# First stage of a hybrid attention layer: wider modulation steps, unmodulated staging of x, and normalization one block ahead

## The chip, the cores and the metric

The kernel runs on one core of a Trainium2 chip. The metric is the device time of one launch in microseconds; smaller is better. The kernel before was timed in three runs: median 3094.35 us, from 3090.94 to 3095.23 us. One further execution was profiled. Engines are named as the profile names them: PE multiplies matrices (PEld loads its stationary operand), DVE, ACT and POOL work element by element, SP issues nearly all transfers (its queue is SPq; ACT has a queue of its own, ACTq).

## The reference

One decoder layer over 2048 tokens of width 1024, in float32:

```
mod = silu(c) @ w_ada + b_ada                    # 6 x 1024 columns: shift_a, scale_a, gate_a, ...
h   = rms_norm(x, g_attn) * (1 + scale_a) + shift_a
proj = h @ w_in                                  # q|k|v of 8 FoX heads, q|k|v of 8 stick-breaking heads, 8 forget logits
...                                              # both attentions, head norms
x = x + gate_a * (mix @ w_out)
...                                              # gated MLP with a width-3 causal convolution
out = rms_norm(x, g_final)
```

The change touches the first three lines alone. For them, `mod` needs only the first 2048 columns of `w_ada` (shift and scale, 8 MB), `h` needs all 1024 features of a token for its norm, and every projection needs `h` of all features.

## The kernel before, in words

Tokens go in four blocks of 512 (`TB`), features in eight tiles of 128 (`KT`; kt counts them). Products are made with operands split in a rounded high part and the remainder (`split`, L43: ACT writes the high part on L44, POOL or DVE the low part on L45), so that one product is three matmuls.

The attention runs over 32 units (kind, pair of heads, token block), `units` on L648: stick-breaking ("sb") pairs first, then FoX. While a unit attends (`attend`), the projection of later units is worked off as a filler, so PE has both kinds of work; `pace` and `follow` set how fast. The four units of ("sb", 0) are special: their projection also makes `h`. `norm_proj` (L417) loads a block of x, normalizes it, transposes it, applies the modulation, splits the result into `hp` tiles, multiplies, and stores `hp` to memory (`hs`) for the other pairs. Block 0 of ("sb", 0) is drained before any attention starts (L770): that is the first stage. The tool that builds the program orders the instructions of each engine itself; each engine then runs its own in that order, and an instruction that waits holds all behind it on its engine. The transfers of SP and ACT together take turns with eight completion semaphores, so each transfer waits for the one that used its semaphore eight transfers earlier.

In the first stage, for each kt in turn:

- `mod_cols(kt)` (L206) loads both 128-column stripes of `w_ada` (L209, two transfers of 512 KB in runs of 512 bytes), scales five of the eight row groups by silu(c) and adds them up on DVE (L212, L214), scales three on ACT (L216) and adds them on POOL (L218); PE sums over the partitions with eight LDWEIGHTS and one-column matmuls (L223), and DVE writes one column each of shift and scale (L224, L225) into `mod_a`.
- `w[1](kt)` loads one 128 x 256 piece of the raw q|k weights through a ring of three buffers (L258, L259) and splits it, the low part on DVE.
- `modulate` (L100) transposes four tiles of x on PE (L114), and ACT reads them from PSUM with the scale and shift of this kt (L119), so these transposes' banks are held until the modulation is known. The split puts `hp`'s low part on DVE in block 0 and on POOL in the later blocks.
- `done` stores `hp` (L430) and adds three matmuls for q and three for k (L284).

After kt 7 come the v weights (L259, L44, L45) and the v product (L355, 96 matmuls in four groups of 24), q and k are copied out of PSUM (L314, L315, L330) and sent to their attention layout by eight transfers (L319, L334). `steps_of_values` (L391) writes v to memory, reads it back shifted by one token (L399), and subtracts.

For blocks 1 to 3, the x loads stand ahead of `modulate` (L658), and the first step of the generator squares (ACT, L95), takes the root (L96), the reciprocal (DVE, L97) and scales (L106) all four tiles, just before that block's transposes.

## Time and profile before

| what | us |
|---|---|
| median of three runs | 3094.35 |
| profiled execution, as timed | 3089.98 |
| its span, first to last instruction | 3088.3 |
| PE busy | 2951.0 |
| DVE busy | 2075.5 |
| ACT busy | 1682.6 |
| POOL busy | 992.2 |

In the profile, "busy" counts an engine's instructions without the waits between them. A row of the timeline gives start, duration, engine, line, operation and, in brackets, how long the engine had been idle and what it waited for. A row of a windows view gives the busy time and the instruction count of PE, PEld, DVE, ACT and POOL in a stretch of time, then the clock that PE was granted (1.00 is full), the busy share of the transfer engines and GB/s. The first query and key matmuls of the attention start at 72.19 us, the transposes of block 1 at 79.19 us, those of block 2 near 121 us and those of block 3 at 185.45 us.

### The profile page before, as it was taken

What the parts mean: (1) busy time and instruction counts of PE and PEld (TensorE: products, weight loads), DVE (VectorE), ACT (ScalarE), POOL (GpSimd) and SP (SyncE); (2) the same over time, 40 slices, a digit from 0 to 9 for tenths busy, and PEclk for the clock granted to TensorE, in tenths of its full rate; (3) what the DMA queues carried; (4) which work ended last, traced back from release to release, by engine and by line L of the source; (5) the groups of instructions that cost most, each with busy time, mean ns of one, the idle gap of its engine ahead of it and who ended that gap; (6) DMA issues with size and microseconds to landing.
All of it is one profiled execution on the core that took longest, in us unless ns stands there. A gap on an engine that the chain in (4) does not pass through costs nothing.

```text
span 3088.3 us, 45418 instructions
## 1 busy us (share of the span) xinstructions
PE 2951.0 (96%) x15934; PEld 2510.9 (81%) x15934; DVE 2075.5 (67%) x3206; ACT 1682.6 (54%) x3129; POOL 992.2 (32%) x1011
## 2 busy tenths in 40 slices
PE   6889999999999999999998999999899998999998
PEld 5788888888888897888876788888688887888887
DVE  6768878887876667578634687778877776254243
ACT  5657767776776656568534444444444444333332
POOL 1531322143122422321123344444444442332331
PEclk8999999999999999999999999999999999999999
DMA  9648756776579855956167522222322224555562
GB/s 272 229 134 293 239 191 202 289 230 202 183 235 341 269 191 184 303 188 224 59 214 226 187 85 82 82 82 76 92 76 82 82 82 155 183 199 167 183 204 86
DMA packets 310614, 546.80 MB, mean 177 GB/s; under 512 B 30737, under 2 KB 187153, under 8 KB 309361
## 3 DMA queue, kind: packets, MB, share of 16 engines
q1 hardware_dynamic: 298752, 531.27, 53.0%
q10 hardware_dynamic: 11632, 12.63, 1.2%
q8 instruction: 126, 2.06, 0.3%
q14 instruction: 104, 0.84, 0.1%
HBM read 407.14 MB, written 130.36 MB: 174 GB/s over the span
## 4 chain that ended last, share of the span: by engine, by line
PE 57%; DMA 12%; DVE 12%; POOL 7%; issue 7%; ACT 4%; SPq 1%; POOLq 0%; ACTq 0%; DVEq 0%
PE ps_pj L284 8%; PE ps_o L1084 8%; PE ps_pv L461 7%; PE ps_pt L452 6%; PE ps_pj L355 5%; PE ps_t L1084 4%; PE ps_bc L1084 4%; PE ps_qk L442 3%; PE ps_o L746 3%; PE ps_o L934 3%; PE ps_qk L443 3%; DMA wuraw<-in_w_up_dram 3%; DVE wu L45 3%; DVE u L1003 2%; POOL wuraw L921 2%
## 5 line engine op out<-in xcount | busy, mean ns | idle before, releaser
L934 PE MATMUL ps_o<-oa,wu 128*128 128x512 f32 x2088 | 504.1, 392 | 11.9 <-DVE oa L45 6.0
L934 PEld LDWEIGHTS ps_o<-oa,wu 128*128 128x128 f32 x2088 | 390.8, 188 | 102.5 <-DVE oa L45 9.8
L457 DVE TENSOR_TENSOR at<-ps_pt,at 128x512 fp32r<-128x512 f32 (+1 forms) x576 | 365.6, 651 | 101.8 <-ACT at L456 98.5
L284 PE MATMUL ps_pj<-hp,w_qk 128*128 128x512 f32 x1512 | 421.1, 406 | 13.3 <-DMA hp<-hs 7.6
L480 DVE TENSOR_TENSOR_SCAN a<-r,a 128x512 f32<-128x512 f32 (+2 forms) x320 | 374.0, 1186 | 86.3 <-POOL a L477 45.1
L461 PE MATMUL ps_pv<-at,V 128*128 128x256 f32 x2304 | 406.3, 293 | 17.4 <-DVE at L457 6.3
L456 ACT ACTIVATE at<-ps_pt 128x512 fp32r<-128x512 f32 (+1 forms) x576 | 318.9, 576 | 157.2 <-PE ps_pt L452 123.6
L461 PEld LDWEIGHTS ps_pv<-at,V 128*128 128x128 f32 x2304 | 335.8, 191 | 54.1 <-DVE at L457 19.7
L284 PEld LDWEIGHTS ps_pj<-hp,w_qk 128*128 128x128 f32 x1512 | 274.5, 191 | 65.4 <-DMA hp<-hs 8.7
L45 DVE TENSOR_TENSOR wd<-wdraw,wd 128x1024 fp32r<-128x1024 f32 x88 | 114.1, 1297 | 261.6 <-ACT wd L44 261.5
L442 PE MATMUL ps_qk<-K,Q 128*128 128x512 f32 (+2 forms) x640 | 264.7, 414 | 11.4 <-ACT a L475 6.0
L1084 PE MATMUL ps_o<-wd,g 128*128 128x512 f32 x1040 | 250.7, 391 | 8.7 <-ACT g L44 8.7
L45 POOL TENSOR_TENSOR g<-graw,g 128x512 fp32r<-128x512 f32 x84 | 144.6, 1722 | 323.4 <-ACT g L44 309.3
L934 PE MATMUL ps_t<-ob,wu 128*128 128x512 f32 x984 | 241.6, 390 | 0.0
L355 PE MATMUL ps_pj<-w_v,hp 128*128 128x256 f32 (+1 forms) x1536 | 237.1, 290 | 2.6 <-DVE w_v L45 1.3
L44 ACT ACTIVATE wu<-wuraw 128x512 fp32r<-128x512 f32 x214 | 133.2, 626 | 190.7 <-PE ps_o L934 120.5
L1084 PEld LDWEIGHTS ps_o<-wd,g 128*128 128x128 f32 x1040 | 196.1, 189 | 49.9 <-ACT g L44 9.1
L443 PE MATMUL ps_qk<-K,Q 128*128 128x512 f32 (+2 forms) x640 | 236.1, 370 | 0.0
L355 PEld LDWEIGHTS ps_pj<-w_v,hp 128*128 128x128 f32 x1536 | 211.8, 192 | 12.4 <-DVE q L315 2.1
L934 PEld LDWEIGHTS ps_t<-ob,wu 128*128 128x128 f32 x984 | 185.4, 188 | 38.7
L44 ACT ACTIVATE wd<-wdraw 128x1024 fp32r<-128x1024 f32 x88 | 93.1, 1058 | 206.2 <-PE ps_bc L1084 190.9
L474 ACT ACTIVATE r<-ps_qk 128x512 f32<-128x512 f32 (+2 forms) x320 | 172.5, 540 | 60.4 <-PE ps_qk L443 58.4
(222 smaller groups left out, 5504.3 us busy)
## 6 DMA issues: line engine op xcount, KB each, us to landing
hp<-hs SPq DMA_DIRECT2D x224, 512.0 KB
wuraw<-in_w_up_dram SPq DMA_DIRECT2D x84, 512.0 KB
wdraw<-in_w_down_dram SPq DMA_DIRECT2D x84, 512.0 KB
g<-u SPq DMA_DIRECT2D x42, 512.0 KB
graw<-g SPq DMA_DIRECT2D x84, 256.0 KB
hs<-hp SPq DMA_DIRECT2D x32, 512.0 KB
hp<-in_w_ada_dram SPq DMA_DIRECT2D x32, 512.0 KB
qk_fox<-q SPq DMA_DIRECT2D x32, 512.0 KB
```

The costliest lines, as they stand in the source:

```text
L44: nc.scalar.activation(hi, src, AF.Copy)
L45: (lo_engine or nc.gpsimd).tensor_sub(lo, src, f(hi))
L284: nc.tensor.matmul(acc, w[kt][:, a, n], h[:, bb], start=kt == 0 and i == 0, stop=kt == KT - 1 and i == 2)
L355: nc.tensor.matmul(av[:, t * width:(t + 1) * width], hts[kt][:, a, tok], w[1][kt][:, bb, 0:width], start=kt == 0 and m == 0, stop=kt == KT ...
L442: nc.tensor.matmul(b[:, :cw], Q[:, hl, 0, qcols], K[:, hl, :cw], start=True, stop=False)
L443: marks.append(nc.tensor.matmul(b[:, :cw], Q[:, hl, 1, qcols], K[:, hl, :cw], start=False, stop=True).ins)
L456: nc.scalar.activation(at[:, 0, lo:], b[:, lo:], AF.Copy)
L457: nc.vector.tensor_sub(at[:, 1, lo:], b[:, lo:], f(at[:, 0, lo:]))
L461: nc.tensor.matmul(o[:, 0:2 * P], V[kt // 4][:, kt % 4, hl, :], rhs, start=first and kk == 0 and w == 0, stop=last and kk == 1 and w == 1)
L480: nc.vector.tensor_tensor_scan(rev, r[:, 0:need][:, ::-1], rev, 0.0 if right[qi] is None else right[qi][:, 0:1], ALU.mult, ALU.add)
L934: nc.tensor.matmul(b, w[:, p, j], o[:, q], start=first and i == 0, stop=last and i == 2, skip_group_check=True)
L1084: nc.tensor.matmul(banks[t][n], g[:, a, t * P:(t + 1) * P], w[:, b, n * TB:(n + 1) * TB], start=k == 0 and i == 0, stop=k == NKD - 1 and i ...
```

## The change

Block 0 gets a function of its own, `first_block`, and the normalization of block n+1 is started inside block n.

- **Modulation in four steps.** `load_ada(g)` loads 256 columns each of shift and scale in eight transfers of 256 KB with runs of 1024 bytes; the first two of four groups have eight own buffers, the third sits in the two Q buffers, the fourth in two `at` and two `q2` buffers. `mod_cols(g)` scales three row groups on ACT (L256), adds them on POOL (L258), and DVE adds the other five onto that sum (L261). There are four one-column matmuls per step, and shift and scale of two kt at once.
- **All loads up front.** The loads of x, all of `w_ada`, the raw q|k weights, the raw v weights (both in V buffers) and x of block 1 are written in a row, none waiting for a buffer of the first stage. The small loads of `wfr` and `b_fgate` move from SP's queue to ACT's.
- **x staged unmodulated.** All 32 transposes of block 0 are copied to SBUF (K buffers) as they are, on ACT and DVE in turn (L468, L466); ACT applies the modulation from there (L476).
- **Low parts.** The low parts of the first pair's weights move from DVE to POOL; in blocks 1 to 3, every second `hp` low part moves from POOL to DVE.
- **Late stores.** The `hp` tiles of block 0 are stored after the stage: three behind the k transfers, five behind the read-back of v.
- **Normalization ahead.** `begin_block(tb + 1)` loads and normalizes the next block; for block 1 behind the v weights, for blocks 2 and 3 behind the last step of `modulate` of the block before.

The core of the diff:

```diff
+    def begin_block(tb, step=TB // P):
+        xts = load_x(tb)
+        junk = f(sb.tile([P, 2, 2 * 2 * P], F32R, name="at", tag="at", bufs=3)).rearrange("p a n -> p (a n)")
+        normalize(px, xts, "a", junk, step)
+        blocks.append(xts)
...
+            for k in range(2):
+                r = (2 * m + k) * P
+                nc.sync.dma_start(w[:, k], w_ada[r:r + P, 0:2 * D].rearrange("p (i n) -> p i n", i=2)[
+                    :, :, g * 2 * P:(g + 1) * 2 * P])
...
+    nc.scalar.dma_start(wfr, w_in[:, 6 * 512:6 * 512 + NH].rearrange("(k p) n -> p k n", p=P))
+    for t in range(4):
+        nc.scalar.dma_start(bf_c[t * NH:(t + 1) * NH], b_fgate.rearrange("o n -> n o"))
+    begin_block(0, 1)
+    load_ada(0)
+    raw_qk = load_raw(3 * 512, 4)
+    raws = {"qk": next(raw_qk)}
+    load_ada(1)
+    next(raw_qk)
+    load_ada(2)
+    load_ada(3)
+    raw_v = load_raw(3 * 512 + 1024, 1)
...
-    def mod_cols(kt):
-        w = sm.tile([P, KT, 2, P], F32, name="ada", bufs=3)
-        for i in range(2):
-            nc.sync.dma_start(w[:, :, i], w_ada[:, i * D + kt * P:i * D + (kt + 1) * P].rearrange(
-                "(k p) n -> p k n", p=P))
...
+    def mod_cols(g):
+        w = [adas[4 * g + k // 2][:, k % 2] for k in range(KT)]
+        for k in range(3):
+            nc.scalar.activation(w[k], w[k], AF.Copy, scale=cs[:, k:k + 1])
+            if k:
+                nc.gpsimd.tensor_add(w[0], w[0], w[k])
+        t = sm.tile([P, 2, 2 * P], F32, name="adas", bufs=1)
+        for k in range(3, KT):
+            nc.vector.scalar_tensor_tensor(t, w[k], cs[:, k:k + 1], w[0] if k == 3 else t, ALU.mult, ALU.add)
...
+    def first_block(w):
+        xts = blocks[0]
+        stage = [sb.tile([P, 2, TB], F32, name="xT", tag="K", bufs=5) for _ in range(KT // 2)]
+        for kt in range(KT):
+            b = pt()
+            for i, xt in enumerate(xts):
+                nc.tensor.transpose(b[:, i * P:(i + 1) * P], xt[:, kt * P:(kt + 1) * P], ident)
+            if kt % 2:
+                nc.vector.tensor_copy(stage[kt // 2][:, kt % 2], b)
+            else:
+                nc.scalar.activation(stage[kt // 2][:, kt % 2], b, AF.Copy)
+        aq, ak = pj(), qk()
+        hts = []
+        for kt in range(KT):
+            w[1](kt)
+            if kt % 2 == 0:
+                mod_cols(kt // 2)
+            hf = px.tile([P, TB], F32, name="hf_a", bufs=2)
+            nc.scalar.activation(hf, stage[kt // 2][:, kt % 2], AF.Identity, scale=mod_a[:, 0, kt:kt + 1],
+                                 bias=mod_a[:, 1, kt:kt + 1])
+            h = h_tile()
+            split(h[:, 0], h[:, 1], hf, nc.vector)
+            hts.append(h)
+            accumulate(aq, 0, w[0], h, kt)
+            accumulate(ak, 1, w[0], h, kt)
+        w[1:] = [w[2]()]
+        begin_block(1)
+        g = finish_proj("sb", 0, 0, aq, w, hts, ak)
+        next(g)
+        with tc.issue_after(copied[-1]):
+            for kt in range(3):
+                nc.sync.dma_start(hs[0][kt], f(hts[kt]))
+        drain(g)
+        with tc.issue_after(fetched[-1]):
+            for kt in range(3, KT):
+                nc.sync.dma_start(hs[0][kt], f(hts[kt]))
...
+        yield
+        yield from modulate(px, pt, blocks[tb], mod_a, lambda kt: h_tile(), done, "a", True)
+        if tb + 1 < NTB:
+            begin_block(tb + 1)
+        yield from finish_proj("sb", 0, tb, aq, w, hts)
```

Three places of the order that the change makes, each before and then now.

**ACT's first instructions** (`rows`: gains and biases; `wfr`, `bf_c`: the small loads; `at<-xt` on L95: the square of a tile of x; names in brackets: what is waited for, DMAHW being the eight completion semaphores). Before:

```order
L196 DMA rows_306<-in_g_out_fox_dram 4x128
L196 DMA rows_306<-in_g_out_sb_dram 4x128
L196 DMA rows_306<-in_b_ada_dram 48x128 [waits DMAHW1_49]
L95 ACTIVATE at_333,ss_a_334<-xt_315 128x1024 [waits DMAHW2_49]
L96 ACT_TABLE_LOAD [waits DVE_49]
L96 ACTIVATE ss_a_334<-ss_a_334,epsc_275 128x1 [waits Activation_49]
L95 ACTIVATE at_333,ss_a_339<-xt_316 128x1024 [waits DMAHW4_49]
```

Now:

```order
L229 DMA rows_306<-in_g_out_sb_dram 4x128
L229 DMA rows_306<-in_b_ada_dram 48x128 [waits DMAHW1_49]
L231 DMA wfr_312<-in_w_in_dram 128x8x8 [waits DMAHW3_49]
L233 DMA bf_c_282<-in_b_fgate_dram 8x1 [waits DMAHW5_49]
L233 DMA bf_c_282<-in_b_fgate_dram 8x1 [waits DMAHW7_49]
L233 DMA bf_c_282<-in_b_fgate_dram 8x1 [waits DMAHW1_49]
L233 DMA bf_c_282<-in_b_fgate_dram 8x1 [waits DMAHW3_49]
L95 ACTIVATE at_326,ss_a_327<-xt_318 128x1024 [waits DMAHW2_49]
L256 ACTIVATE ada_347<-ada_347,cs_279 128x512 [waits DMAHW2_49,Activation_49]
```

Five transfers, each with a wait for an earlier transfer, now stand ahead of ACT's first square; they left SP's queue, where they stood ahead of the first `w_ada` load.

**ACT around the last `hp` tiles of block 0** (`hf_a`: modulated x; `hp`: its high part; `w_v`: the split of the v weights; `at<-xt`: squares of block 1). Before:

```order
L119 ACTIVATE hf_a<-ps_pt,mod_a 128x512
L44 ACTIVATE hp<-hf_a 128x512
L216 ACTIVATE ada<-ada,cs 128x256 x3
L95 ACTIVATE at,ss_a<-xt 128x1024
L455 ACTIVATE at<-edge 128x2x128 x2
L95 ACTIVATE at,ss_a<-xt 128x1024
L119 ACTIVATE hf_a<-ps_pt,mod_a 128x512
L95 ACTIVATE at,ss_a<-xt 128x1024
L44 ACTIVATE hp<-hf_a 128x512
L95 ACTIVATE at,ss_a<-xt 128x1024
```

Now:

```order
L476 ACTIVATE hf_a<-xT,mod_a 128x512 x2
L44 ACTIVATE w_v<-raws 128x256
L44 ACTIVATE w_v<-wfr 128x8
L44 ACTIVATE w_v<-raws 128x256
L44 ACTIVATE hp<-hf_a 128x512
L95 ACTIVATE at,ss_a<-xt 128x1024
L44 ACTIVATE hp<-hf_a 128x512
L525 ACTIVATE at<-edge 128x2x128 x2
L95 ACTIVATE at,ss_a<-xt 128x1024
L476 ACTIVATE hf_a<-xT,mod_a 128x512 x2
L95 ACTIVATE at,ss_a<-xt 128x1024
L44 ACTIVATE hp<-hf_a 128x512 x2
```

The v weights, of which six stand ahead of the first row shown, and three squares of block 1 now come ahead of kt 6 and 7.

**PE at the end of the first stage** (`ps_pj<-w_v,hp`: the v product; `ps_qk<-K,Q`: the first attention matmuls). Before:

```order
L355 MATMUL ps_pj<-w_v,hp 128x264 x39
L442 MATMUL ps_qk<-K,Q 128x256
L443 MATMUL ps_qk<-K,Q 128x256
L442 MATMUL ps_qk<-K,Q 128x256
L443 MATMUL ps_qk<-K,Q 128x256
L355 MATMUL ps_pj<-w_v,hp 128x264 x48
```

Now:

```order
L325 MATMUL ps_pj<-hp,w_qk 128x512 x2
L325 MATMUL ps_qk<-hp,w_qk 128x512 x2
L396 MATMUL ps_pj<-w_v,hp 128x264 x73
L512 MATMUL ps_qk<-K,Q 128x256
L513 MATMUL ps_qk<-K,Q 128x256
```

The first attention matmuls stood between two halves of the v product; they now follow all of it.

More of the change, by code (lines that the diff above doesn't have):

```diff
@@ new lines @@
+    wfr = sm.tile([P, KT, NH], F32, name="wfr")
+    nc.scalar.dma_start(wfr, w_in[:, 6 * 512:6 * 512 + NH].rearrange("(k p) n -> p k n", p=P))
[10 more added lines that the diff above has]
+    raw_v = load_raw(3 * 512 + 1024, 1)
+    raws["v"] = next(raw_v)
@@ L768, in first_out @@
         yield from out_proj(0, mix0, lambda: halves.pop(0), lambda: bank(psc, "bc", 2), [])
[L770 removed]
+    weights["sb", 0], results["sb", 0] = load_w("sb", 0), []
+    first_block(weights["sb", 0])
     load_unit(*units[0], results["sb", 0])
```

137 lines of the change are left out of this document (67 added, 70 removed).

## The prediction

> **What bounds the kernel now.** I read the page first, then windows by stage, then the chain of waits of the first stage.
>
> ```profile
> span 3088.3 us, 45418 instructions
> PE 2951.0 (96%) x15934; PEld 2510.9 (81%) x15934; DVE 2075.5 (67%) x3206; ACT 1682.6 (54%) x3129; POOL 992.2 (32%) x1011
> 0.00:60.00 60.00, 38.62 (x152) 29.82 (x153) 39.19 (x95) 37.74 (x82) 14.18 (x22) 0.84 1.02 303
> 60.00:80.00 20.00, 16.78 (x109) 15.90 (x108) 9.37 (x27) 6.61 (x22) 0.88 (x3) 0.80 0.56 138
> 80.00:260.00 180.00, 160.75 (x1025) 139.64 (x1023) 128.81 (x178) 115.53 (x244) 78.98 (x73) 0.96 0.60 204
> 260.00:320.00 60.00, 60.00 (x351) 51.86 (x350) 48.74 (x64) 42.71 (x84) 3.63 (x7) 1.00 0.83 278
> ```
>
> PE is busy for 2951.0 us, 96% of the span, so time can only be won where it is not. Of its 137 us of idle time 21.4 lie before 60 us, 3.2 before 80 and 19.25 between 80 and 260; from there to 320 it is never idle, so what is won before 260 us should reach the end whole. The first stage also runs at a low granted clock (0.84, 0.80), so its busy time is stretched.
>
> ```profile
> 2.93 5.34 DMA rows<-in_g_out_fox_dram
> ...
> 11.66 7.19 DMA ada<-in_w_ada_dram
> ...
> 20.93 6.49 DMA ada<-in_w_ada_dram
> ...
> 31.86 7.26 DMA ada<-in_w_ada_dram
> ...
> GB/s 0 150 388 361 382 77 140 332 293 292 290 291 291 289 293 291 313 372 306 290 360 337 291 294 291 310 392 405 342 304 360 403 415 403 402 412 205 164 184 143
> ```
>
> The chain of the first stage is loads of `w_ada`. The last row gives the traffic of its first 64 us in slices of 1.6 us: x comes in by 8 us, there is a hole (77, 140), then 290 GB/s while `w_ada` and raw weights come in runs of 512 bytes, and 403 to 415 near 50 us, where x and the `hp` stores move in runs of 4 KB. So transfers bound this stage.
>
> **The loads.** Ahead of the end of the stage now stand x (2.1 MB), `w_ada` (8.4), q|k (1.05), v (1.05) and x of block 1 (2.1); the `hp` stores (4.2 MB) are gone from it. No row shows runs of 1024 bytes. Bounds are 290 and 405 GB/s; I take 340, nearer the shorter run. From the end of x at 8 us to the sixth piece of v (10.2 MB), for which ACT waits in its order, that is 43 us, 33 us, and 38 us as I take it.
>
> **ACT starts later.** This is the price of moving the small loads.
>
> ```profile
> 5.16 1.06 ACT L95 ACTIVATE at<-xt 128x1024 f32<-128x1024 f32 x1 [1.95 <-DMA xt<-in_x_dram]
> 5.58 3.32 SPq L231 DMA_DIRECT2D bf_c<-in_b_fgate_dram  x4
> 8.94 1.02 SPq L209 DMA_DIRECT2D ada<-in_w_ada_dram  x2
> ```
>
> SP spent 5.58 to 8.90 on four tiny loads, waiting for earlier transfers (the chain's first row ends at 8.27). These waits now stand ahead of ACT's first square. It started at 5.16; it cannot start before 8.27, and the last of the four also waits for `wfr`, so I take 10.5. SP can issue `w_ada` from about 5.2, which closes the hole.
>
> **ACT's work up to the last `hp` tile**, by rows:
>
> ```profile
> 6.33 1.28 ACT L96 ACT_TABLE_LOAD   x1
> 7.82 1.04 ACT L95 ACTIVATE at<-xt 128x1024 f32<-128x1024 f32 x1
> 9.19 1.04 ACT L95 ACTIVATE at<-xt 128x1024 f32<-128x1024 f32 x1
> 34.39 0.71 ACT L44 ACTIVATE w_qk<-raw_qk 128x256 fp32r<-128x256 f32 x2
> 45.59 0.40 ACT L44 ACTIVATE w_v<-raw_v 128x256 fp32r<-128x256 f32 x1
> 45.99 0.41 ACT L44 ACTIVATE w_v<-raw_v 128x256 fp32r<-128x256 f32 x1
> 82.69 1.18 ACT L44 ACTIVATE hp<-hf_a 128x512 fp32r<-128x512 f32 x2
> 53.11 0.71 ACT L455 ACTIVATE at<-edge 128x256 fp32r<-128x256 f32 x2
> ```
>
> A square with its root takes 1.37 from start to start, without the root about 1.2. Four and three of these are 9.1; the table load 1.3; eight q|k pieces at 0.36, 2.8; eight v pieces with their forget columns at 0.40, 3.2; the edge copies 0.7; and 32 operations of 128x512 (12 scalings of `w_ada`, 4 staging copies, 8 modulations, 8 high parts) at 0.59, 18.9. Sum 36.0: without any wait the last high part ends at 46.5. Behind the sixth v piece stand 10 us of it (four modulations and four high parts 4.7, three squares 3.6, rest 1.5), so arrival at 38 us gives 48. The modulations also wait for DVE's columns: 1 us for each of the last three groups, taken from the groups' turns on DVE behind the low parts. I take **51**, with 46.5 and 55 as ends. POOL's added work in the stage (eight adds, 16 weight splits) ends ahead of it.
>
> **From the last `hp` tile to the end of v.**
>
> ```profile
> 58.06 0.61 ACT L44 ACTIVATE hp<-hf_a 128x512 fp32r<-128x512 f32 x1
> 61.69 0.60 ACT L44 ACTIVATE q<-ps_qk 128x512 fp32r<-128x512 f32 x1 [0.26 <-PE ps_qk L284]
> 62.04 1.41 DVE L106 TENSOR_SCALAR xt<-xt,ss_a 128x1024 f32<-128x1024 f32 x2
> 63.77 0.68 DVE L315 SCALAR_TENSOR_TENSOR q<-ps_pj,q 128x512 fp32r<-128x512 f32 x1
> 63.83 6.43 PE L355 MATMUL ps_pj<-w_v,hp 128*128 128x264 f32 x35 [1.30 <-DVE w_v L45]
> 72.19 0.35 PE L442 MATMUL ps_qk<-K,Q 128*128 128x256 f32 x1 [1.93 <-issue]
> 72.74 6.03 PE L355 MATMUL ps_pj<-w_v,hp 128*128 128x264 f32 x48
> 79.19 1.03 PE L114 MATMUL ps_pt<-edge,xt 128*128 128x128 f32 x8
> ```
>
> From the end of the last high part (58.7) to the copy of k took 3.0, so the products end at 54. A wait appears here: v's second group needs the PSUM bank of q, and q's low part stands on DVE behind four scalings of block 1: fourth square and root to 52.5, reciprocal 0.2, scalings 2.8, copies of v's first group 0.6, low part 0.7, which is 56.8. Queued behind it on PE are 72 v matmuls at 0.126 (6.03 for 48), 9.1; the 35 that began cold took 0.184, 2.0 more in all, which I charge again. v ends at **67.9** (ends 63.4 and 71.9) where it ended at 78.8: **10.9 won** (15.4, 6.9). The q and k transfers took 64.5 to 72.2 and now fit under v.
>
> **Blocks 1 to 3.**
>
> ```profile
> 86.83 2.41 POOL L400 TENSOR_TENSOR hp<-hp 128x1024 f32<-128x1024 f32 x1
> 91.66 1.66 PE L284 MATMUL ps_pj<-hp,w_qk 128*128 128x512 f32 x6 [1.03 <-POOL hp L45]
> 100.52 0.62 ACT L44 ACTIVATE hp<-hf_a 128x512 fp32r<-128x512 f32 x1
> 185.45 0.47 PE L114 MATMUL ps_pt<-edge,xt 128*128 128x128 f32 x1 [4.85 <-DVE xt L106]
> 180.00:200.00 20.00, 15.15 (x79) 13.04 (x80) 14.04 (x19) 14.56 (x27) 12.10 (x12) 0.74 0.38 145
> ```
>
> - Block 3 waits 4.85 for its normalized x, and the clock falls to 0.74. Normalized a block ahead, that wait should go: +5 (0 to 7, with the clock).
> - PE waits for POOL's low parts (1.03 here, another like it near 125): +1.5 (0 to 3) for half of them on DVE.
> - The first attention matmuls came 6.6 us before v's end and their ACT, POOL and DVE steps lay under v. Now they follow it: -2 (0 to -6.6).
> - The last five stores of block 0 hold `hp` buffers (ten in the ring) that block 1 wants. v came back 8 us after its product's end; five stores of 512 KB at 405 GB/s are 6.5, so all are out some 14.5 behind v's end, while block 1's last high part came 21.7 behind it. -1 (0 to -3).
>
> Sum 10.9 + 5 + 1.5 - 2 - 1 = 14.4, against the profiled execution of 3089.98 (span 3088.3, 1.7 around it): 3075.6. The median of the runs is 4.4 above that execution, so against it the forecast is 3094.35 - 14.4, **3080 us**.
>
> **Rivals.**
>
> - *Longer runs are no faster (chance 0.17).* `w_ada` still comes at 290 GB/s. Then v ends at 71.9 and the sum is 6.9 + 3.5: 3084. Against it speaks that 4 KB runs reach 405. The Trainium skill (DMA: Bandwidth & Descriptors, Specifications) says that runs of 512 bytes and more already go at line rate, which is this case; by the rows above, 512 bytes did not.
> - *Nothing waits (0.15).* ACT's 36 us run dense, 15.4 are won, and the blocks give their upper ends less a little: 22, **3072**. For it: 405 GB/s near 50 us. Against: ACT waited for DVE's modulation columns in every kt.
> - *The attention sets the pace (0.10).* Between 80 and 260 PE waits for sigmoids, selects and scans; if that chain governs, only the shift of the first attention matmuls counts, 72.2 to 68: 4 us, 3090, within what can be told. For it: the 19.25 us of PE's idle time there. Against it: the projections fill that time to 89%.
> - *The out-projection stalls (0.06).* Its PE order (L746, L837) changes too, with transposes placed elsewhere among the matmuls.
>
> ```profile
> PE ps_t L837 <- DVE x L833: 5.0, 2, 4.4
> ```
>
>   The longest single wait is 4.4. If each of seven later units there met one such wait, 31 us in place of these 5.0, 26 would be lost: 3106. It decides from 14.4 us of added waits on. Against it: tiles are normalized a unit ahead in both orders, and the transposes move later as often as earlier.
>
> **How the numbers follow.** My forecast has 0.52. What a measurement can tell from no change is 0.2%, 6.2 us. The first three cases but for their tails are faster: 0.82. The attention's case and tails are the same: 0.11. Slower: 0.07. Range: the fast rival and the bounds' upper ends (25 won) set 3067; at the other end 6.9 won and half the losses, 3 us won, 3091.
>
> **What would show it.** Right: ACT's first square near 10.5; `w_ada` traffic between 320 and 360 GB/s; the last `hp` of block 0 near 51; q's low part near 56; v's end near 68 with the first attention matmuls right behind; no wait of several us for L104 ahead of block 3's transposes; from 260 us of before on, the same stages some 14 us earlier. Wrong: a first square before 8 us; v's end beyond 75; PE idle for over 20 us between v's end and block 3; a PE idle sum beyond 320 us that differs by more than 5 from before.

## The result, and the profile after

| | median us | lowest to highest | runs |
|---|---|---|---|
| before | 3089.71 | 3085.48 to 3095.42 | 12 |
| changed | 3091.28 | 3087.62 to 3101.36 | 12 |

The ratio is 1.0006, with an interval from 0.9994 to 1.0018: no change that can be measured. The forecast was 3080, faster. It was taken from the first three runs of the kernel before (3094.35); with twelve runs that median is 4.6 lower, so the forecast's 14.4 would mean 3075.3. The profiled execution of the changed kernel took 3093.19 us.

Page and windows by stage of the changed kernel, to be laid beside those of the kernel before (busy time of PE, PEld, DVE, ACT and POOL with counts, then clock, transfer share and GB/s):

```profile
span 3091.5 us, 45281 instructions
PE 2944.7 (95%) x15902; PEld 2501.1 (81%) x15902; DVE 2079.9 (67%) x3174; ACT 1680.7 (54%) x3121; POOL 986.4 (32%) x1015
0.00:60.00 60.00, 32.60 (x117) 25.05 (x118) 37.49 (x60) 38.06 (x81) 30.53 (x38) 0.89 0.80 253
60.00:80.00 20.00, 18.74 (x128) 16.65 (x127) 9.88 (x22) 6.82 (x18) 2.53 (x5) 0.98 0.64 185
80.00:260.00 180.00, 161.14 (x1030) 140.24 (x1031) 137.18 (x188) 116.29 (x242) 64.25 (x60) 0.97 0.65 223
20.00:40.00 20.00, 14.61 (x53) 11.92 (x54) 18.47 (x27) 12.07 (x25) 13.61 (x12) 1.00 1.10 340
```

The span is 3.2 longer, PE's busy time 6.3 shorter, so its idle time is 9.5 longer: 146.8. Of that, +6.0 lies before 60 us, -2.0 from 60 to 80, -0.4 from 80 to 260, none from there to 320, and +5.8 beyond. The loads came as forecast (340 GB/s in the last row, and from 40 to 60 us the transfers are mostly idle: share 0.37, where it was 1.00 before). So loads no longer bound the stage, and it still did not become 10.9 us shorter. What bounds it now is seen in the timeline of ACT, DVE and PE, put together:

```profile
11.10 1.06 ACT L95 ACTIVATE at<-xt 128x1024 f32<-128x1024 f32 x1 [7.87 <-DMA bf_c<-in_b_fgate_dram]
...
25.34 1.09 ACT L468 ACTIVATE xT<-ps_pt 128x512 f32<-128x512 f32 x2 [2.68 <-PE ps_pt L464]
...
30.20 1.52 ACT L476 ACTIVATE hf_a<-xT,mod_a 128x512 f32<-128x512 f32 x2 [2.86 <-DVE mod_a L269]
...
38.26 1.52 ACT L476 ACTIVATE hf_a<-xT,mod_a 128x512 f32<-128x512 f32 x2 [2.40 <-DVE mod_a L269]
...
47.90 1.52 ACT L476 ACTIVATE hf_a<-xT,mod_a 128x512 f32<-128x512 f32 x2 [2.81 <-DVE mod_a L269]
...
55.34 1.52 ACT L476 ACTIVATE hf_a<-xT,mod_a 128x512 f32<-128x512 f32 x2 [1.48 <-DVE mod_a L269]
56.76 1.04 ACT L95 ACTIVATE at<-xt 128x1024 f32<-128x1024 f32 x1
...
57.80 1.13 ACT L44 ACTIVATE hp<-hf_a 128x512 fp32r<-128x512 f32 x2
...
65.17 0.68 DVE L356 SCALAR_TENSOR_TENSOR q<-ps_pj,q 128x512 fp32r<-128x512 f32 x1
...
65.40 9.03 PE L396 MATMUL ps_pj<-w_v,hp 128*128 128x264 f32 x72 [0.68 <-DVE hp L405]
74.34 0.36 PE L512 MATMUL ps_qk<-K,Q 128*128 128x256 f32 x1
```

ACT waits for the modulation columns in all four groups, 9.55 us in all, and for PE's first transposes of x another 2.68. It also squares one more tile of block 1 between the last modulation and its high parts. These waits, 12.23 in all, and a first square 0.6 later account for the last `hp`: the prediction's dense order ended at 46.5, which makes 59.3. The last `hp` ends at 58.9, where it did before (58.7). v ends at 74.3: 4.3 to 4.5 earlier than before, not 10.9.

Why the columns are late stands in the rows of DVE and POOL:

```profile
38.87 1.54 DVE L261 SCALAR_TENSOR_TENSOR adas<-ada,cs,adas 128x512 f32<-128x512 f32 x2
47.77 5.16 DVE L261 SCALAR_TENSOR_TENSOR adas<-ada,cs,adas 128x512 f32<-128x512 f32 x4
...
45.11 1.17 POOL L45 TENSOR_TENSOR w_v<-raws,w_v 128x256 fp32r<-128x256 f32 x1
46.25 0.20 POOL L45 TENSOR_TENSOR w_v<-wfr,w_v 128x8 fp32r<-128x8 f32 x1
46.41 0.73 POOL L45 TENSOR_TENSOR w_v<-raws,w_v 128x256 fp32r<-128x256 f32 x1
47.10 0.69 POOL L45 TENSOR_TENSOR w_v<-wfr,w_v 128x8 fp32r<-128x8 f32 x1
47.76 0.73 POOL L45 TENSOR_TENSOR w_v<-raws,w_v 128x256 fp32r<-128x256 f32 x1
48.44 0.65 POOL L45 TENSOR_TENSOR w_v<-wfr,w_v 128x8 fp32r<-128x8 f32 x1
```

The same sum step takes 0.77 while POOL is idle and 1.29 while POOL splits the v weights; POOL's 128x8 step goes from 0.20 to 0.65 or 0.69, while its 128x256 step beside it stays at 0.73. One sum of DVE and one pair of POOL steps both take 1.29 there, as if they took turns. Part of the work that the change moved from DVE to POOL comes back as longer DVE steps: in the last group 5.16 for four steps that take 3.08 with POOL idle, 2.1 us.

In block 1 a wait is new (PE, ACT and SP's queue):

```profile
91.12 4.27 PE L325 MATMUL ps_pj<-hp,w_qk 128*128 128x512 f32 x10 [5.84 <-POOL hp L45]
86.84 0.63 ACT L44 ACTIVATE hp<-hf_a 128x512 fp32r<-128x512 f32 x1 [4.26 <-DMA hs<-hp]
81.60 4.90 SPq L493 DMA_DIRECT2D hs<-hp  x5
```

ACT wants an `hp` buffer at 82.6 and must wait for a late store; POOL's low part and ten products stand behind it.

Last, a table of marks: the start of the last product of some groups (v of blocks 0 and 3 of the first pair, then v of later units, then the last product with V, and the last matmul of the kernel). First row: us in the kernel before; the others: difference to it; before_again and after_again are further executions of the two programs, the rest are the experiments below (in the last two the marks between are left out, since work was moved across them). Each row is a single profiled execution, while the times of the experiments are medians of several runs; e5's, e6's and e13's profiled executions were the longest of their runs, e11's and e12's the shortest.

```
                    v0     v3    773    883   1051   1111   1265  lastV    end
before             78.6  233.0  772.7  882.9 1051.0 1111.0 1264.9 1545.7 3080.0
before_again       -0.6   -0.3   -4.4   -4.4   -4.7   -4.6   -2.0   -0.8   -3.3
after_again        -5.6   -4.6   -3.5   -2.2   -1.9   +0.4   +2.2    0.0   +0.4
after              -4.3   -4.1   -4.0   -3.8   -3.4   +1.9   +2.0   +3.6   +3.2
e1_stores          -5.3   -7.9   -5.2   -4.9   -1.1   +1.1   +3.3   +4.1   +4.6
e2_pe_terms        -5.5   -7.6   -5.4   -5.5   -5.7   -2.8   -2.1   -1.9   -1.0
e3_small           -6.4   -6.1   -3.4   -3.3   -1.9   +1.6   +2.1   +2.9   +3.0
e4_before_norm     +0.1   -0.1   -3.2   -3.0   -4.0   -5.8   -4.9   -3.5   +0.2
e5_chain           -4.7   -6.1   -0.5   -0.3   -0.1   +5.5   +8.7   +9.1  +13.0
e6_no_modulation  -29.1  -31.2  -34.0  -33.7  -32.0  -30.4  -31.7  -30.9  -30.4
e7_both            -8.1  -12.0   -8.5   -8.0   -8.3   -3.3   -2.5   -2.6   -2.1
e8_ring            -7.0   -9.7   -9.1   -8.5   -8.1   -3.1   -2.5   -2.3   -0.9
e9_before_nomod   -29.9  -27.3  -28.1  -28.1  -26.6  -24.9  -25.1  -26.2  -27.9
e10_both_light     -6.7   -9.4  -18.6  -18.6  -20.3  -36.5  -20.0  -21.3  -17.0
e11_before_light   +0.3   +0.3  -10.6  -11.3   -4.5  -17.5  -11.1  -14.1  -16.6
e12_both_early     -8.0  -11.3                                     -12.2  -13.4
e13_before_early   -0.1    0.0                                      +3.0   +3.1
```

Of the changed kernel's lead, 4.1 stood at the end of v of block 3. It was kept to 1051 us and gone 60 us later. There the profiles of before and of the change show (PE, and SP's queue):

```profile
1068.49 3.94 SPq L305 DMA_DIRECT2D K<-qk_fox  x4
1072.48 2.11 SPq L410 DMA_DIRECT2D hp<-hs  x3
...
1078.41 2.93 PE L284 MATMUL ps_pj<-hp,w_qk 128*128 128x512 f32 x6 [2.12 <-DMA hp<-hs]
```

```profile
1068.57 5.20 SPq L346 DMA_DIRECT2D K<-qk_fox  x4
1073.82 1.71 SPq L451 DMA_DIRECT2D hp<-hs  x3
...
1079.64 2.93 PE L325 MATMUL ps_pj<-hp,w_qk 128*128 128x512 f32 x6 [5.99 <-DMA hp<-hs]
```

PE came 2.6 us earlier to the place where it needs reloaded `hp` tiles (1073.65 for 1076.29), and the tiles came 1.2 later. The transfers are busy there (share 0.99 from 1060 to 1080 in both kernels). From the end of v of block 3 to the out-projection both programs have the same instructions in the same order on every engine; so this loss is no reordering.

### The profile page after: what moved, and what is told of

Read it like the earlier page. It is cut to its first block, busy times and chain, and to the rows that moved or that the text cites. A ratio compares the mean times of both kernels' runs of the same rounds, so it can differ in the third digit from the quotient of the medians.

```text
span 3091.5 us, 45281 instructions
## 1 busy us (share of the span) xinstructions
PE 2944.7 (95%) x15902; PEld 2501.1 (81%) x15902; DVE 2079.9 (67%) x3174; ACT 1680.7 (54%) x3121; POOL 986.4 (32%) x1015
## 3 DMA queue, kind: packets, MB, share of 16 engines
q1 hardware_dynamic: 289712, 531.24, 52.5%
## 4 chain that ended last, share of the span: by engine, by line
PE 54%; DMA 13%; DVE 12%; POOL 8%; issue 8%; ACT 4%; SPq 1%; POOLq 0%; ACTq 0%; DVEq 0%
PE ps_pj L325 9%; PE ps_o L1155 8%; PE ps_pv L531 7%; PE ps_pt L522 6%; PE ps_pj L396 4%; PE ps_t L1155 4%; PE ps_o L1005 4%; PE ps_bc L1155 4%; DMA wuraw<-in_w_up_dram 3%; PE ps_qk L512 3%; PE ps_qk L513 3%; DVE wu L45 3%; DMA r<-rstd 2%; DVE u L1074 2%; POOL ws L993 2%
```

## The experiments

Each time is a median, set beside the median of the kernel before in the same study; the ratio is to that kernel too, with its 95% interval in brackets.

### The first stage's chain

**Small loads behind the raw weights** (e3_small):

```diff
-    nc.scalar.dma_start(wfr, w_in[:, 6 * 512:6 * 512 + NH].rearrange("(k p) n -> p k n", p=P))
-    for t in range(4):
-        nc.scalar.dma_start(bf_c[t * NH:(t + 1) * NH], b_fgate.rearrange("o n -> n o"))
...
     next(raw_v)
...
+    nc.sync.dma_start(wfr, w_in[:, 6 * 512:6 * 512 + NH].rearrange("(k p) n -> p k n", p=P))
+    for t in range(4):
+        nc.sync.dma_start(bf_c[t * NH:(t + 1) * NH], b_fgate.rearrange("o n -> n o"))
```

> The changed kernel with the five small loads (wfr, bf_c) behind the raw weights in SP's queue, ahead of x of block 1, in place of ACT's queue. Theory (they hold ACT's first square, and all behind it, by 6 us): the first square starts near 5.2 in place of 11.1, the first modulation near 25 in place of 30.2, and v of block 0 ends some 4 us earlier, near 70. Rival (behind the first group the sums wait for w_ada and for DVE, so that ACT's early start is lost): the first square and the first modulation move, but the last modulation stays within 1.5 us of 55.3 and v of block 0 within 1.5 us of 74.3.

Three rows of ACT's timeline:

```profile
5.12 1.06 ACT L95 ACTIVATE at<-xt 128x1024 f32<-128x1024 f32 x1 [1.89 <-DMA xt<-in_x_dram]
...
26.97 1.52 ACT L476 ACTIVATE hf_a<-xT,mod_a 128x512 f32<-128x512 f32 x2 [5.75 <-DVE mod_a L269]
...
53.59 1.50 ACT L476 ACTIVATE hf_a<-xT,mod_a 128x512 f32<-128x512 f32 x2
```

ACT's first square starts 6.0 earlier, the first modulation 3.2, the last 1.75, and v of block 0 ends 2.1 earlier (the marks). Each step of the chain swallows part of the lead: ACT's late start cost about 2 us, between the 4 of the theory and the 1.5 of the rival; the rest was waiting for the columns anyway. Time: 3092.16 against 3091.77, ratio 1.0003 (0.9991 to 1.0015).

**Three of eight terms as products on PE** (e2_pe_terms) takes ACT's scalings and POOL's adds out of the modulation:

```diff
-            nc.scalar.activation(w[k], w[k], AF.Copy, scale=cs[:, k:k + 1])
-            if k:
-                nc.gpsimd.tensor_add(w[0], w[0], w[k])
+                nc.tensor.matmul(e[:, i:i + 1], w[k][:, i // 2, i % 2 * P:(i % 2 + 1) * P], cs[:, k:k + 1],
+                                 start=k == 0, stop=k == 2)
```

> The changed kernel with three of the eight terms of each modulation sum as products on PE (w_ada against a column of c) in place of three scalings on ACT and two adds on POOL, so that DVE's sum no longer waits for ACT and POOL; 12 scalings, 8 adds less, 48 products of one column more. Theory (the stage's bound is the chain ACT, POOL, DVE of each group, and DVE and POOL slow each other): the scaled sums on DVE go from 0.95 to 1.75 us each towards 0.75 where POOL is idle, the last modulation of block 0 starts near 48 in place of 55.3, and v of block 0 ends near 68 in place of 74.3. Rival 1 (ACT's and DVE's work is the bound, the chain is not): the last modulation starts after 53, v ends after 72. Rival 2 (the added products of one column on a cold PE, some 0.2 us each and two passes, take the place of what is won): PE has no idle time between 40 and 60, and v ends at 74 or later. Behind it as in the first run: a lead of some 6 us that is carried, or is lost near 1075.

DVE twice, then PE:

```profile
35.23 1.54 DVE L265 SCALAR_TENSOR_TENSOR adas<-ada,cs,adas 128x512 f32<-128x512 f32 x2
...
43.00 3.88 DVE L265 SCALAR_TENSOR_TENSOR adas<-ada,cs,adas 128x512 f32<-128x512 f32 x3
...
54.49 0.95 PE L268 MATMUL ps_pv<-ones,adas 128*128 128x1 f32 x8
```

With POOL idle the sums take 0.77, with POOL's weight splits beside them (39.3 to 49.4 us) 1.29: the sizes of the changed kernel, in another arrangement. The last sum is ready at 46.9, but its one-column products stand on PE behind q and k products of kt 4 and 5 and ten v products, and run at 54.49. The last modulation started at 56.14, later than in the changed kernel (55.34). The chain left ACT and POOL and took up PE's queue: v ended at 73.2, 1.1 earlier in place of the theory's 6. The first rival's signs came (a last modulation after 53, v after 72), by another cause than it named. Time: 3088.14, ratio 0.9991 (0.9978 to 1.0005).

**The next group's sum a step ahead** (e5_chain, with e3's and e1's edits; sums in place, the squares of block 1 held back):

```diff
+        mod_cols(0, mod_sum(0))
         for kt in range(KT):
             w[1](kt)
-            if kt % 2 == 0:
-                mod_cols(kt // 2)
+            if kt % 2 == 0 and kt < KT - 2:
+                mod_cols(kt // 2 + 1, mod_sum(kt // 2 + 1))
...
+        with tc.issue_after(last.ins):
+            begin_block(1, xts=xt1)
```

> The changed kernel with e1's stores in the loop and e3's small loads behind the weights, and three more edits of the first stage: each group's sum goes into its first scaled tile in place of a tile of its own, so that it does not wait for PE to have read the one before; the sum and the columns of group g+1 stand ahead of the modulation and products of group g; the squares of block 1 stand behind the last high part of block 0. Theory (the last modulation is late because of the order of a chain ACT, POOL, DVE, PE, DVE that runs once for each group): the last modulation starts near 49 in place of 55.3 (e3: 53.6), v of block 0 ends near 68 (e3: 72.3) and v of block 3 near 220 (e1: 225.1). Rival (work is the bound, not order: POOL and DVE slow each other): the last modulation after 52.5 and v of block 0 after 71. Behind it: e1 and e3 had leads of 7.9 and 6.1 us over the kernel before at the end of v of block 3 and none at the end. If a lead leaks away bit by bit and at the reloads near 1075, the marks from 1113 on are again within 3 us of before's and the time is 0.999 to 1.0005 of before's. If only those orders lost it, the time is 0.996.

DVE, then PE:

```profile
60.14 2.74 DVE L104 TENSOR_SCALAR xt<-xt,ss_a 128x1024 f32<-128x1024 f32 x4
62.79 0.68 DVE L359 SCALAR_TENSOR_TENSOR q<-ps_pj,q 128x512 fp32r<-128x512 f32 x1
...
63.53 10.57 PE L399 MATMUL ps_pj<-w_v,hp 128*128 128x264 f32 x72 [2.56 <-DVE q L359]
```

The last modulation starts at 51.94 and k is copied at 60.27 (64.66 in the changed kernel), but q's low part waits behind the four scalings of block 1, PE stands still for 2.56, and the 72 v products run at a lower granted clock (0.84 for 1.00 in the changed kernel): 10.57 for 9.03. v ends at 74.0. The last modulation comes before the rival's 52.5 but short of the theory's 49; v ends after 71, as the rival had it. The chain was shortened by 4 us up to the copy of k, and the next wait took them. Time: 3091.07, ratio 1.0008 (0.9994 to 1.0022); its profiled execution, the row of the marks, was its longest, 3103.05.

### The waits of blocks 1 to 3

**The stores back in the loop** (e1_stores), with the x loads of block 1 issued ahead of them:

```diff
+        xt1 = load_x(1)
         for kt in range(KT):
...
             accumulate(aq, 0, w[0], h, kt)
+            nc.sync.dma_start(hs[0][kt], f(h))
             accumulate(ak, 1, w[0], h, kt)
...
-        with tc.issue_after(copied[-1]):
-            for kt in range(3):
-                nc.sync.dma_start(hs[0][kt], f(hts[kt]))
```

> The changed kernel with the stores of the first block's h put back into the loop over kt, right behind each low part; x of block 1 is loaded ahead of that loop, so that its transfers keep their place in SP's queue. Marks in the changed kernel: v of blocks 0 to 3 ends at 74.3, 118.1, 168.6 and 228.9 us; v products end at 1047.7 and 1113.0; the last product with V is at 1549.3 (before: 78.6, 119.8, 167.1, 233.0; 1051.0, 1111.0; 1545.7). Theory (the late stores hold the ring of hp buffers): PE's wait of 5.84 us in block 1 for the low part of POOL goes, v of block 1 ends near 111, of block 3 near 222. Rival (the stores only move the wait: they now stand ahead of the transfers of q and k): the first attention products come later than 74.3 by 3 us or more, and v of block 3 ends within 2 us of 228.9. What becomes of a lead behind it: if it is carried, all marks to the end come 6 to 7 us earlier and the time is 0.998 of after's; if the reloads of h near 1075 us come at their own time, the wait there grows from 6.0 to 12 or so and the marks from 1113 on stay within 2 us of after's.

PE's timeline:

```profile
87.48 4.64 PE L325 MATMUL ps_pj<-hp,w_qk 128*128 128x512 f32 x10 [3.63 <-POOL hp L45]
```

The wait of 5.84 is gone; one of 3.63 for POOL's low part stays. v of block 1 ends at 114.4 (118.1 in the changed kernel), v of block 3 at 225.1 (228.9). Of these 3.7 one stood at the end of v of block 0 already, so the late stores cost about 3 us in block 1, three times what was forecast and half of what the theory here expected (block 1 near 111, block 3 near 222). At the end nothing of it is left (+4.6): 3091.97, ratio 1.0008 (0.9995 to 1.0021).

**Normalization a block ahead, alone, in the kernel before** (e4_before_norm):

```diff
+        if tb + 1 < NTB:
+            blocks.append(load_x(tb + 1))
+            normalize(px, blocks[tb + 1], "a", junk(), TB // P)
         yield from finish_proj("sb", 0, tb, aq, w, hts, ak)
```

> The kernel before with one part of the change alone: each x block is loaded and normalized as soon as the transposes of the block ahead of it are issued. Theory (block 3's wait of 4.85 us with its cold clock goes, nothing takes its place): v of block 3 ends near 228 in place of 233.0, and this lead of 5 us is there up to 1051. Rival (the normalization only moves the wait, since its squares on ACT and scalings on DVE now stand ahead of attention work): v of block 3 ends within 2 us of 233.0. Behind it: carried to the end (3089.7 becomes 3085), or lost near 1075, with a wait for h there of 7 us in place of 2.1 and the same end as before.

Windows of two stretches, first of the kernel before, then of this one:

```profile
125.00:175.00 50.00, 47.33 (x316) 41.01 (x314) 38.94 (x55) 29.62 (x63) 23.30 (x20) 1.00 0.62 204
175.00:235.00 60.00, 51.39 (x338) 46.57 (x338) 41.24 (x59) 40.05 (x83) 25.94 (x26) 0.91 0.41 130
```

```profile
125.00:175.00 50.00, 44.61 (x295) 39.64 (x293) 40.27 (x54) 32.91 (x67) 22.39 (x19) 0.97 0.58 189
175.00:235.00 60.00, 54.56 (x371) 48.42 (x371) 46.09 (x62) 40.00 (x88) 31.56 (x28) 1.00 0.46 146
```

The 4.85 wait and the cold clock behind it are gone from the second stretch, and the first, into which the squares and scalings moved, has lost as much: v of block 2 ends 6 later (173.1 for 167.1), v of block 3 at the same time (232.9 for 233.0). Time: 3094.14, ratio 1.0008 (0.9997 to 1.0019). The wait was worth nothing by itself.

### Is a lead carried to the end?

**The modulation's loads and sums left out**, in the changed kernel with e3's and e1's edits (e6_no_modulation) and in the kernel before (e9_before_nomod):

```diff
-    mb = pv()
-    def mod_cols(g):
...
+    nc.vector.tensor_copy(mod_a[:, 1], cols[:, R_BA:R_BA + KT])
+    nc.vector.tensor_copy(mod_a[:, 0], gba)
```

> The first stage of e1 and e3 with the sums over w_ada left out: no load of w_ada for the first modulation, no scalings, adds and sums (scale and shift of the first norm are then those of a zero c, so h and all behind it have other values). All other work and its order from block 1 on is that of the changed kernel. It gives a lead of known size: v of block 0 should end near 45 in place of 74, v of block 3 near 198 in place of 233.0, a lead of 30 us or more over before. Theory 1 (a lead is carried but for some 8 us that are lost at the reloads of h and in small waits): the time is 22 to 27 us under before's, 0.991 to 0.993. Theory 2 (a lead is carried whole, the losses so far were of those orders): 30 us and more, 0.990 or less. Theory 3 (something with a time of its own behind 900 us takes up every lead): less than 8 us, above 0.997.

> The kernel before with the sums over w_ada left out, as in e6: scale and shift of the first norm are those of a zero c, and h and all behind it have the values of e6. Theory A3 (the values decide: with these the chip runs the stretch behind block 3 faster, and e6 hid a loss by that): the stretch takes 1300 to 1306 us where before takes 1312. Rival (the values are of no matter): 1309 to 1313, and the time falls by what the first stage falls, some 25 us.

A lead of 31.2 at the end of v of block 3 is 30.4 at the end of the kernel (3057.53 against 3089.97, ratio 0.9898, 0.9881 to 0.9914). In the kernel before, 27.3 become 27.9 (3062.29, ratio 0.9918, 0.99 to 0.9936). So nothing later sets the end by itself. The values do not set the pace either: from v of block 3 to the last product with V e9 takes 1313.8 with other values, the kernel before 1312.7.

**Both programs once more** (after_again, before_again), unedited:

> The changed kernel again, unedited, for a second profile: it shows how much the marks of one kernel differ from one execution to the next. If the stretch from the v products that end at 1047.7 to those that end at 1113.0 takes 65 us again (60 in before), the loss there belongs to the kernel; if it takes 60 to 62, it belongs to that one execution.

> The kernel before again, unedited, for a second profile: v of blocks 0 and 3 end within 0.3 us of 78.6 and 233.0; if the stretch from 1051.0 to 1111.0 takes 60 us again and PE's wait for h near 1078 is 2 us again, the shorter wait belongs to this kernel; if the wait is 4 to 6, it varies from one execution to the next.

Windows of the kernel before, first execution and second:

```profile
740.00:760.00 20.00, 17.05 (x120) 16.08 (x119) 15.00 (x20) 13.52 (x30) 5.37 (x7) 0.91 0.37 110
```

```profile
740.00:760.00 20.00, 18.70 (x148) 17.83 (x147) 15.96 (x25) 16.77 (x38) 4.94 (x7) 1.00 0.38 107
```

The same program differs here by 1.65 us of PE time in 20 us and a clock of 0.91 or 1.00, and by 4.4 at the mark of 773: a single profile can't tell leads below some 4 us from nothing. One place is steadier: from mark 1051 to 1111, the five executions without the new sums (before, its repeat, e4, e6, e9) take 60.0, 60.1, 58.2, 61.6 and 61.7, the eight with them (the change, its repeat, e1, e2, e3, e5, e7, e8) 62.3 to 65.6. Over the whole way from v of block 3 to the last product with V the two sets stand further apart: 1309.4 to 1313.9 without, 1317.4 to 1327.9 with.

**Both repairs at once** (e7_both: e3's and e1's edits) and the same with the buffer ring of `at` turned by one place (e8_ring):

```diff
     load_ada(3)
+    sb.tile([P, 2, 2, 2 * P], F32, name="ada", tag="at", bufs=3)
```

> e1 and e3 together: stores in the loop over kt, small loads behind the raw weights, nothing else; the control for e8. From e1 (225.1) and e3 (226.9) v of block 3 should end near 223 (before: 233.0). From there to the last product with V the two profiles of before took 1312.7 and 1312.1 us, e4 1309.3 and e6 1312.9; all kernels with the new sums over w_ada took 1317 to 1328, though order and waits of all engines are the same there. Theory A (something in the kernels with the new sums lasts beyond the stage): the stretch takes 1317 to 1328 again, and the time is within 0.1% of before's. Theory B (chance of the executions): near 1311, and the time is 9 us under before's, 0.997.

> e7 with one tile more taken from the ring of three at buffers behind the borrowed ones, and never written: the sums borrow two of three buffers there, so that from block 1 on each attention tile lies one place further in the ring than in the kernel before and in e6; with the third the places are as before. Instructions, order and waits stay. Theory A1 (the places of the attention tiles in SBUF make the difference behind block 3): the stretch from v of block 3 to the last product with V takes 1309 to 1313 us and the time is 6 to 9 us under e7's. Rival A2 (the places are of no matter): 1317 to 1328 as e7, and the same time as e7 within 0.1%.

The lead at v of block 3 is 12.0 (the forecast's size but for its last 2.4), at the end of the profile 2.1, in time nothing: 3089.31 against 3089.52, ratio 1.0004 (0.9994 to 1.0014). With the ring turned: 9.7, 0.9, and 0.9993 (0.9983 to 1.0003). So the place of the attention tiles in the `at` ring is not the cause, and a lead of the forecast's size is lost as the small one is.

### The late loads

The other four parts of `w_ada` are loaded later, from unit 12 on (`late_mod`, 32 transfers of 512 KB), between the reloads of `hp` tiles. In the changed kernel eight of them are issued from 649 to 736 us, eight from 1024 to 1103, the rest up to 1340: the second group lies where the lead goes. The first lies between the v products that end at 544 and at 773 in the kernel before; there the five executions without the new sums take 223.6 to 228.3, the eight with them 227.4 to 230.1. Not all of the loss can be theirs: of e7's 12.0, 3.0 are gone by the mark at 544, before the first of these loads is issued at 643. **28 of these left out**, with e7's edits (e10_both_light) and in the kernel before (e11_before_light):

```diff
             for kt in range(KT):
+                if kt:
+                    yield
+                    continue
                 w = wide()
                 nc.sync.dma_start(w, w_ada[kt * P:(kt + 1) * P, part * D:(part + 1) * D])
```

> e7 with 28 of the 32 loads of w_ada in the late modulation left out, and their scalings and adds with them (the second norm and the gates then have other values; some 15 MB of transfers between 650 and 1340 us are gone). Theory (the lead of the new first stage is lost to transfers that come late in the crowded stretches near 720 and 1050 to 1111 us): with less traffic the stretch from v of block 3 to the last product with V takes the same time as in e11 within 2 us, and the lead of 12 us at v of block 3 is there at the end: e10's time is 10 to 12 us under e11's. Rival (the loss has nothing to do with the traffic there): the stretch takes 7 to 10 us longer than in e11, and the times are equal within 3 us.

> The kernel before with the same 28 loads, scalings and adds left out: the base for e10. v of block 3 ends near 233 as before; PE's waits for reloads of h (7.6 and 9.2 us in the two profiles of before) should fall to under 3, and the stretch to the last product with V to about 1300 to 1306 us.

From v of block 3 to the last product with V, e10 takes 1300.8 and e11 1298.2; with all loads it was 1322.1 (e7) and 1312.7 (before). So of a difference of 9.4 between the two lines 2.6 are left, and of e10's 9.7 lead over e11 at block 3, 7.2 stand at the last product with V. The medians are 3071.51 and 3076.54 (ratios 0.9938, 0.9918 to 0.9957, and 0.9958, 0.9938 to 0.9978), 5.0 apart, against 0.2 between e7 and the kernel before; the theory had 10 to 12, the rival less than 3. In the two profiled executions the 7.2 are lost again in the MLP (0.4 at the end); the medians say that this isn't the rule. So most of the loss up to the last product with V is bound to these loads and the work that hangs on them; the two were not separated. How they cost it is not shown: behind block 3, PE's waits for reloaded `hp` tiles are 10.7 in e7 and 7.6 in the kernel before, which is 3.1 of the difference of 9.4, and they are still 8.2 in e10 and 5.8 in e11, where under 3 was expected.

**The same work three units earlier**, again with e7's edits (e12_both_early) and in the kernel before (e13_before_early):

```diff
-    LATE, PER = 12, 3
+    LATE, PER = 9, 3
```

> e7 with the late modulation and the folding of w_out started three units earlier (unit 9 in place of 12), nothing left out: their transfers move from the stretch of 880 to 1000 us, where the DMA engines are busy all the time, to 720 to 880, where their share is 0.45. Theory (crowded transfers behind block 3 take the lead away): v of block 3 ends near 221 to 223 as in e7, the stretch from there to the last product with V takes under 1315 us, and the time is 6 to 14 us under before's (0.9955 to 0.998). Rival (the late modulation only moves its crowd, and meets the reloads of the earlier units): the stretch takes 1317 us or more, and the time stays within 0.1% of before's.

> The kernel before with the late modulation three units earlier, as in e12. Theory: what e12 wins over this kernel is the lead of its first stage, 10 to 12 us at v of block 3, and 6 us or more of it in the times. Rival: both take the same time within 3 us, so that any gain of e12 is the late modulation's alone.

e12 is the one version with nothing left out that is faster than the kernel before: 3081.05 against 3088.72, ratio 0.9976 (0.9963 to 0.9989). The loads of `w_ada` are issued from 485 to 599 and from 905 to 1215 us, and those of `w_out`, which the same edit moves, from 697 to 890 in place of 811 to 997 (e7). From v of block 3 to the last product with V it takes 1311.8 (e7: 1322.1), e13 1315.7 (the kernel before: 1312.7). The medians of e12 and e13 (3086.76, ratio 0.9990, 0.998 to 1.0001) are 5.7 apart. The theory asked for 6 or more, the rival for less than 3. Their profiled executions are 11.3 apart at v of block 3 and 16.5 at the end, but these are e12's shortest and e13's longest run.

So about half of the first stage's lead comes out in the times once the late work is moved. The edit is worth 2 us in the kernel before (within its interval) and about 8 on top of e7's edits, which were timed in the study before (3089.31). Why it helps is open. It did not move the loads out of busy transfers: one group is now issued from 905 to 984 us, where the transfer share is 1.01; from 1019 to 1098, where e7 issues it, it was 0.83.

## Why the forecast was wrong, point by point

- *ACT's first square at 10.5, `w_ada` at 340 GB/s*: right, 11.10 and 340. The hole behind x was closed.
- *Last `hp` at 51*: it ended at 58.9. This is the step that failed first, with 3 us for "the modulations also wait for DVE's columns". They waited 9.55, and the staging of x waited 2.68 for its transposes, a term that the sum did not have. ACT's own work was sized right: 46.5 without any wait, 0.6 of late start and 12.23 of waits make 59.3. The rows show two reasons for the columns. POOL's weight splits, which I let end "ahead of it", stretch DVE's sums from 0.77 to 1.29. And one chain runs through ACT, POOL, DVE, PE, DVE and ACT four times with little ahead of each turn. How the 9.55 divide between the two was not measured. No bound reached 58.9: the upper one, 55, took the waits at a few us.
- *Products end at 54, q's low part done at 56.8, v at 67.9*: k was copied at 64.66, q's low part was done at 65.85, v ended at 74.3. From the last `hp` to the copy of k it took 5.7 for 3.0, since low parts and products of two tiles stood behind it in place of one; the 72 v products took 9.03 for 9.1, and the 2.0 charged for a cold start did not come (granted clock 1.00 there). 4.5 won in place of 10.9; e2, e3 and e5 reached 72.3 to 74.0, each with a new wait in the place of the shortened one.
- *Block 3's wait, +5*: the wait is gone as told, and worth nothing (e4): the same squares and scalings stand in block 2 and cost 6 there. The rival of the attention's pace, put at 0.10, describes blocks 1 to 3 better in that PE's idle time from 80 to 260 us went from 19.25 to 18.86. Its mechanism is not shown, though: the first attention matmuls came 2.15 later, not 4 earlier, and v of block 3 still ended 4.1 earlier.
- *Late stores, -1*: about -3 (e1). I compared their end with block 1's last high part; ACT wants a buffer 8 us behind the end of v, for an earlier tile.
- *Low parts on DVE, +1.5, and the later attention matmuls, -2*: no run takes these apart. PE's waits for POOL's low parts from 80 to 260 us grew from 2.2 to 7.4, 5.84 of it the wait behind the late stores.
- *"What is won before 260 us should reach the end whole"*: this failed in the changed kernel (4.1 to less than nothing) and in e7 (12.0 to 2.1), though the order behind is the same. It holds for a lead of 30 (e6, e9). The prediction looked at PE's idle time up to 320 us and not at the late `w_ada` work behind it. That this work decides about most of the loss is shown as far as e10 to e13 go. Why the kernels with the new sums take 2 to 6 us more between 1051 and 1111 than the kernel before, and 5 to 15 more from v of block 3 to the last product with V, with the same order of instructions, stays open. Values (e9) and the place in the `at` ring (e8) were ruled out; PE's wait at one reload differs, 2.12 and 5.99, but varies between executions too (2.22 and 4.13 in the repeats).
- The signs named ahead: of those for wrong, one came: the idle sum beyond 320 us differs by 5.8. v's end at 74.3 missed the 75 that would have shown the first stage wrong, and was no sign of right either.
- The range: the 25 us that were to set its lower end lead from 3094.35 to 3069, not to 3067.

The net of the forecast's 14.4: 10.9 became 4.5, +5 became 0, -1 became about -3. At v of block 3 the lead was 4.1, and that was lost behind 1051 us. That the measured median, 3091.28, lies next to the slow end of the range, 3091, is luck: that end stood for 3 us won and carried, and nothing was carried.

## What to carry to other kernels

A stage that is freed from its loads is as long as its dependent chain through the engines: count the turns of the chain and what stands ahead of each turn in every in-order queue, since each shortened link here exposed the next one (e2, e3, e5). An idle time worth removing is one whose work then runs in some other idle time; moved into a busy block it costs there what it saved (e4). A lead of ten microseconds is not safe because the order of instructions behind it stays the same: here 12.0 became 2.1, and about half of such a lead came out in the times after other work, 250 us and more behind it, had been moved (e12). So look through the whole span before adding gains up, and time a lead of known size (e6) or the same lead with later work left out (e10) or moved (e12), beside the kernel before with the same edit.

## What was unexpected of the hardware

- DVE and POOL slow each other when both run steps with two inputs from SBUF: DVE's 128x512 sum 0.77 to 1.29, POOL's 128x8 step 0.20 to 0.69, or its 128x256 step 0.73 to 1.17 (the row at 45.11, which overlaps a sum). The Trainium skill (GPSIMD Engine Reference, Specifications) says that POOL shares its interfaces to SBUF with DVE and that the two contend where DVE has two SBUF inputs or runs in a two-port mode; the traces agree and give the size.
- A short wait of PE may cost more than its length: behind the 2.50 us wait near 743 us of the kernel before the clock was 0.91 over 20 us; in the repeat the longest wait there was 0.85 and the clock 1.00. In e5, 72 products behind a wait of 2.56 took 10.57 for 9.03, at a clock of 0.84. That the wait lowered the clock is inferred from these two pairs.
- Executions of one program with the same order differ by some 4 us at a mark in the middle and meet again later (before and its repeat: 4.7 at 1051, 0.8 at the last product with V).
